# Where the squares of a sublayer's output are summed, and how many feature blocks the sample columns share an operation

## The chip, the cores and the metric

The kernel runs on one core of one Trainium2 chip. Its time is the device time of one launch in microseconds (us), taken as the median of a few runs. PE is TensorE (matrix products), DVE is VectorE, ACT is ScalarE, POOL is GpSimd, SP is SyncE, which only issues transfers here. PSUM is the memory that TensorE writes its products into.

## The reference, cut to what matters

The program is one inference step of a two-layer decoder of width 1024, over a prompt of 512 tokens and a sample group of 8 sequences of 4 tokens. Each layer is a mixer and a convolutional feed-forward network (FFN); around each of these four sublayers stand two RMS norms:

```python
h = _rmsnorm(x, ng[0]) * (1 + sc1) + sh1        # before the sublayer
y, ... = _mixer_ab(h, ...)                      # or _mixer_cd, or _conv_ffn
x = x + g1 * _rmsnorm(y, ng[1])                 # after it
```

`_rmsnorm` multiplies by `rsqrt(mean(x * x, axis=-1) + EPS)`: the mean runs over the 1024 features of a token. `sh1`, `sc1`, `g1` (and three more for the FFN) are one vector for the prompt and one for each sample sequence, so sample columns need another factor than prompt columns.

## The kernel before, in words

Activations lie feature-major: a tile has 128 partitions (features of one of KB = 8 feature blocks), two token halves h = 0 and 1, and HT = 272 columns in each (256 prompt columns and 16 sample columns). A sum over features is therefore a sum over partitions and blocks; it is made by a matmul with `onesD`, a 128x128 matrix whose entries make the mean.

Every large product is made of three matmuls of 272 columns per 128x128 weight block: high part by high part (L618), high weight by low activation (L620), low weight by high activation (L622). `gemm` takes most output blocks with both token halves in one (`ps`, two PSUM banks, two such buffers). At the first blocks after a norm ("lead") and the last blocks of a sublayer ("tail") it goes through half h = 0 of all of them first, and then through h = 1, so that the norm of one half can run beside the products of the other. Of the halved blocks those with number 1, 3 and 6 use a `ps` buffer (in the trace `psmm`), the others a single-bank buffer `p1` (`psmh`), of which there are three. Mixer 0 has four halved tail blocks, FFN 0, mixer 1 and FFN 1 have eight each.

The end of a sublayer is called a junction here. It goes like this for each half:

- `out_evac` takes a block from PSUM. In the FFNs DVE adds it to the partial sum `Yf` (L686). ACT squares it (L694, the first block L689), the square is added to `yacc` (L696): on DVE for blocks of half 0, on POOL for blocks of half 1 and for blocks of both halves. ACT multiplies the prompt columns by the gate (L697), DVE the 16 sample columns (L698).
- `postres` makes one matmul of `yacc` with `onesD` into `psn` (L491). ACT and DVE make 1/sqrt of it (`nr`, L494 to L497), and DVE multiplies the output by it and adds the residual, two blocks per operation (L539, L540).
- `premod` prepares the next sublayer: ACT squares X (L506), eight matmuls sum the squares into `psn` (L491), ACT and DVE multiply by the scale (L518, L519), and after `nr` DVE multiplies by it (L523), adds the shift to the sample columns (L524), ACT writes the rounded high part `Hhi` (L526 for prompt columns, L527 for sample columns) and DVE the low part `Hlo` (L529, L531). The loop takes CH = 2 blocks at a time.

The fourth junction, after the last FFN, has no `premod` behind it; its second half ends the program.

The instruction order on each engine comes from a scheduler that takes the program text, its dependences and the buffers; `tc.issue_after(x)` keeps what is inside behind instruction x. `evacuate` puts each `out_evac` behind the newest weight load. What matters for the order is thus which buffer a matmul needs and what frees it: a block can't start until an earlier block of its buffer has been read by DVE or ACT.

Of the kernel before, what the change touches and what calls it, by code (L numbers as in the profile page):

```python
# [13 lines left out]
P = 128  # L14
# [5 lines left out]
HT = 272  # L20
# [247 lines left out]
def build(nc, tc, ctx, t):  # L268
# [214 lines left out]
        w = np_.tile([P, 1], F32, name="warm")  # L483
        A.activation(w, x, AF.Abs_reciprocal_sqrt, bias=epsb)

    def rstd(parts, ones):

        ps = pp.tile([P, 512], F32, name="psn", tag="pn", bufs=1)[:, :HT]
        n = len(parts)
        for i, a in enumerate(parts):  # L490
            PE.matmul(ps, ones, a, start=(i == 0), stop=(i == n - 1))  # L491
        r = np_.tile([P, HT], F32, name="nr", bufs=2)
        q = np_.tile([P, HT], F32, name="nq", bufs=2)
        A.activation(r, ps, AF.Abs_reciprocal_sqrt, bias=epsb)  # L494
        V.scalar_tensor_tensor(q, r, -0.5, r, op0=M, op1=M)
        V.scalar_tensor_tensor(q, ps, EPS, q, op0=ADD, op1=M)
        V.scalar_tensor_tensor(r, q, 1.5, r, op0=ADD, op1=M)  # L497
        return r

    CH = 2  # L500

    def squares(h):
        parts = []
# [6 lines left out]
    def premod(l, s, h, tmp):  # L510

        ca, sh = cA[l][s], mods[l][:, 24 * s:24 * s + 8, :]
        parts = squares(h)
        ws = []
        for c in range(0, KB, CH):
            w = tmp(c, CH)
            for k in range(CH):
                A.activation(w[:, k, 0:256], X[:, c + k, h, 0:256], AF.Copy, scale=ca[:, c + k, 0:1])  # L518
            V.tensor_tensor(s44(w), s44(X[:, c:c + CH, h, :]), bmod(ca, c, c + CH, h), op=M)  # L519
            ws.append(w)  # L520
        r = rstd(parts, onesD)
        for w, c in zip(ws, range(0, KB, CH)):
            V.tensor_tensor(w, w, r.unsqueeze(1).to_broadcast([P, CH, HT]), op=M)  # L523
            V.tensor_tensor(s44(w), s44(w), bmod(sh, c, c + CH, h), op=ADD)  # L524
            for k in range(CH):
                A.activation(Hhi[:, c + k, h, 0:256], w[:, k, 0:256], AF.Identity, bias=sh[:, c + k, 0:1])  # L526
            A.activation(Hhi[:, c:c + CH, h, 256:272], w[:, :, 256:272], AF.Copy)  # L527
            for k in range(CH):
                V.scalar_tensor_tensor(Hlo[:, c + k, h, 0:256], w[:, k, 0:256], sh[:, c + k, 0:1],  # L529
                                       Hhi[:, c + k, h, 0:256], op0=ADD, op1=SUB)  # L530
            V.tensor_tensor(Hlo[:, c:c + CH, h, 256:272], w[:, :, 256:272], Hhi[:, c:c + CH, h, 256:272], op=SUB)  # L531

    def postres(h, Y, acc, out=None):
        r = rstd([acc[:, h, :]], onesD)
        for c in range(0, KB, CH):
            y = Y[:, c:c + CH, h, :]
            x = X[:, c:c + CH, h, :]
            E = G if c in POOLED else V
            E.tensor_tensor(y, y, r.unsqueeze(1).to_broadcast([P, CH, HT]), op=M)  # L539
            E.tensor_tensor(x, x, y, op=ADD)  # L540
            if out is not None:
                SY.dma_start(out[:, c:c + CH, h, :], x)
# [132 lines left out]
    def out_evac(Y, acc, cg, fresh, final):  # L675

        def ev(i, n, ps, h0, h1):
            y, src = Y[:, n, h0:h1, :], ps[:, h0:h1, :HT]
            if not final:
                if fresh:  # L680
                    A.activation(y, src, AF.Copy)
                else:
                    V.tensor_tensor(y, src, y, op=ADD)
                return
            if not fresh:
                V.tensor_tensor(y, src, y, op=ADD)  # L686
                src = y
            if i == 0:
                A.activation(acc[:, h0:h1, :], src, AF.Square)  # L689
                if h0 == 0:  # L690
                    warm(acc[:, 0, 0:1])
            else:
                sq = np_.tile([P, 2, HT], F32, name="nsq2", tag="nsq", bufs=NSQ)
                A.activation(sq[:, h0:h1], src, AF.Square)  # L694
                E = V if h1 == 1 else G
                E.tensor_tensor(acc[:, h0:h1, :], acc[:, h0:h1, :], sq[:, h0:h1], op=ADD)  # L696
            A.activation(y[:, :, 0:256], src[:, :, 0:256], AF.Copy, scale=cg[:, n, 0:1])  # L697
            V.tensor_tensor(y[:, :, 256:272].rearrange("p a (b t) -> p a b t", t=4),  # L698
                            src[:, :, 256:272].rearrange("p a (b t) -> p a b t", t=4),
                            cg[:, n, 1 + 4 * h0:1 + 4 * h1].rearrange("p (a b) -> p a b", b=4).unsqueeze(3)  # L700
                            .to_broadcast([P, h1 - h0, 4, 4]), op=M)
        return ev

    def yacc():
        return np_.tile([P, 2, HT], F32, name="yacc")


    def ffn(l, nxt, side, pre):
        pre()
        es = ExitStack()  # L710
        fp = es.enter_context(pool(f"ffn{l}"))
        ey, Y = ExitStack(), []

        def open_y():
            Y.append(ey.enter_context(pool(f"ffny{l}", side="right")).tile([P, KB, 2, HT], F32, name="Yf"))

        act_hi = fp.tile([P, 7, 2, HT], F32R, name="act_hi")
        act_lo = fp.tile([P, 7, 2, HT], F32R, name="act_lo")
        so = fp.tile([P, FB, 9, 2], F32, name="fso")
        if l == 0:  # L720
            apool.append((fp, ADB[1]))
        exts = [fp.tile([P, 562], F32, name=f"fext{i}") for i in range(FEXT)]
        SY.dma_start(so, t[f"st_f{l}"])
        for e in exts:
            G.memset(e[:, 0:2], 0.0)
        wo, bo = PAR["f_w"][0] + l * 132, PAR["f_b"][0] + l * 44
        acc = yacc()
        zs, live, cnt = {}, {}, [0]

        def up_ev(i, nb, ps, h0, h1):  # L730
            if h0 == 0:
                live[nb] = exts[cnt[0] % FEXT]
                cnt[0] += 1
                fill_state(live[nb], 2, so[:, nb, 1:9])
            ext = live[nb]
            A.activation(fpr(ext, 2, h0, h1), cpr(ps, h0, h1), AF.Copy)  # L736
            V.tensor_copy(fsa(ext, 2, 6, 2, h0, h1), csa(ps, h0, h1))  # L737
            if h1 != 2:
                return
            save_state(ext, 2, so[:, nb])  # L740
            z = fp.tile([P, 562], F32, name="fz", bufs=4)
            conv3(z, ext, par[:, wo + 3 * nb:wo + 3 * nb + 3], par[:, bo + nb:bo + nb + 1])
            zs[nb] = z
            if nb < NF:
                return
            n = nb - NF
            za, zg = zs.pop(n), zs.pop(nb)
            A.activation(zg[:, :560], zg[:, :560], AF.Silu)
            V.tensor_tensor(za[:, :560], za[:, :560], zg[:, :560], op=M)
            hi, lo = act_hi[:, n % 7], act_lo[:, n % 7]  # L750
            split(fpr(za, 0), cpr(hi), cpr(lo))
            split(zsa(za), csa(hi), csa(lo))

        def ups(n0, n1):
            return [x for n in range(n0, n1) for x in (n, NF + n)]

        def up(n0, n1, **k):
            return gemm(ups(n0, n1), srcH, up_ev, **k)

        def down(gi):  # L760
            b0, b1 = FGROUPS[gi]
            fin = gi == len(FGROUPS) - 1
            return gemm(range(KB), lambda k: (act_hi[:, (b0 + k) % 7], act_lo[:, (b0 + k) % 7]),
                        out_evac(Y[0], acc, cG[l][1], gi == 0, fin), tail=TAILF if fin else 0,
                        mids=(None, lambda: junction(0, Y[0], acc, nxt)))

        def body():
            ng = len(FGROUPS)
            yield from up(0, FGROUPS[0][1], lead=LEADF)
            open_y()  # L770
            for gi in range(ng - 1):
                e = FGROUPS[gi][1]
                yield from up(e, e + 1)
                yield from down(gi)
                yield from up(e + 1, FGROUPS[gi + 1][1])
            for i, _ in enumerate(down(ng - 1)):
                if i == 3:
                    with queued():
                        SY.dma_start(t[f"o_f{l}"], so)
                yield  # L780
            del apool[1:]

        weave(body(), side)
        es.close()
        return lambda: (junction(1, Y[0], acc, nxt), ey.close())
# [4 lines left out]
    def mixer0(nxt, side, begun):  # L790
# [1 line left out]
        mp = es.enter_context(pool("mix0"))  # L792
        yhi = mp.tile([P, KB, 2, HT], F32R, name="yhi")
        ylo = mp.tile([P, KB, 2, HT], F32R, name="ylo")
        acc = yacc()
        ea = ExitStack()
        ap_ = ea.enter_context(pool("mix0a"))
        oa = ap_.tile([P, 4, 9, 2], F32, name="oa")
# [98 lines left out]
    def mixer1(nxt, pre):  # L897
        pre()
        es = ExitStack()
        tp = es.enter_context(pool("mix1t"))  # L900
        acc = yacc()
        qs = tp.tile([P, 3, 2, 2, P], F32, name="qs")
        ks = tp.tile([P, 6, 32], F32, name="ks")
        vnew = tp.tile([P, 256], F32, name="vnew")
# [521 lines left out]
```

## Time and profile before

| what | value |
|---|---|
| median of 3 runs | 1440.73 us (1440.14 to 1442.59) |
| profiled execution | 1443.65 us, span of its instructions 1441.6 us |
| mean granted TensorE clock in it | 0.982 of full |
| PE busy | 1378.7 us, 96% of the span |
| DVE busy | 873.6 us, 61% |
| ACT busy | 609.1 us, 42% |
| POOL busy | 117.4 us, 8% |

Busy times are summed over the span, and engines overlap, so they don't add up to it. "Idle before, releaser" in a row is how long the engine stood still ahead of that instruction, and which other engine's instruction let it go on. PEclk is the clock that TensorE was granted as a share of full speed, 2.4 GHz; 0.50 is its lower level, 1.2 GHz. Times in rows with a start count from the start of the span.

### The profile page before, as it was taken

To read this page: it belongs to the slowest core of one execution; us is meant where nothing else is said; L and a number is where in the kernel's file an instruction comes from. 1 tells how busy PE (TensorE), PEld (TensorE's weight loads), DVE (VectorE), ACT (ScalarE), POOL (GpSimd) and SP (SyncE) were. 2 spreads that over 40 slices of the span, in tenths; PEclk is the share of its full clock that TensorE was granted. 3 is DMA by queue.
4 is the path that set the end of the run, shared out by engine and by line. 5 is a ranking of instruction groups with operands and counts; after the bars stand their busy time and mean duration, and the time that the engine had idled before them with its cause. 6 is when DMAs were issued, how large, how long until landed. Compare 5 with 4: busy or idle time off the path is not lost.

```text
span 1441.6 us, 27411 instructions
## 1 busy us (share of the span) xinstructions
PE 1378.7 (96%) x10762; PEld 1281.2 (89%) x10762; DVE 873.6 (61%) x1830; ACT 609.1 (42%) x1148; POOL 117.4 (8%) x354
## 2 busy tenths in 40 slices
PE   6999999999999999998899999899899999999995
PEld 4789998999999999988899998577799999999995
DVE  4743359652554464368689888536886257366467
ACT  4421357442442343257433433536654344244244
POOL 0100012100100010003000000000221011011001
PEclk9999999999999999999999999999899999999998
DMA  9666413344535444442443131554142533655821
GB/s 353 245 206 215 159 61 111 112 147 141 160 95 191 149 138 132 147 158 60 132 94 102 49 112 60 176 208 147 46 129 81 184 116 125 224 192 186 275 83 62
DMA packets 111016, 207.73 MB, mean 144 GB/s; under 512 B 19332, under 2 KB 32132, under 8 KB 110376
## 3 DMA queue, kind: packets, MB, share of 16 engines
q1 hardware_dynamic: 109088, 202.58, 43.2%
q10 hardware_dynamic: 1800, 3.42, 0.7%
q8 instruction: 84, 1.38, 0.4%
q14 instruction: 44, 0.36, 0.1%
HBM read 198.63 MB, written 34.39 MB: 162 GB/s over the span
## 4 chain that ended last, share of the span: by engine, by line
PE 89%; DVE 6%; ACT 2%; DMA 2%; issue 1%; POOL 0%; POOLq 0%; SPq 0%; DVEq 0%; ACTq 0%
PE psmm L618 24%; PE psmm L620 23%; PE psmm L622 23%; PE psada L432 3%; PE psn L491 3%; PE psmh L618 2%; PE psmh L620 2%; PE psmh L622 1%; PE pso L1116 1%; PE psl L1082 1%; PE psl L1084 1%; DVE wlo L559 1%; DVE X L540 1%; DMA kc<-kc 1%; PE pssm L1168 1%
## 5 line engine op out<-in xcount | busy, mean ns | idle before, releaser
L618 PE MATMUL psmm<-Hhi,whi 128*128 128x272 f32 x2028 | 436.3, 292 | 0.0
L622 PE MATMUL psmm<-Hhi,wlo 128*128 128x272 f32 x2028 | 429.4, 289 | 0.0
L620 PE MATMUL psmm<-Hlo,whi 128*128 128x272 f32 x2028 | 428.8, 289 | 0.0
L558 ACT ACTIVATE whi<-wraw 128x512 fp32r<-128x512 f32 (+1 forms) x404 | 234.2, 598 | 389.6 <-PE psmm L620 349.8
L559 DVE TENSOR_TENSOR wlo<-wraw,whi 128x512 fp32r<-128x512 f32 (+1 forms) x404 | 257.1, 651 | 202.1 <-ACT whi L558 194.4
L618 PEld LDWEIGHTS psmm<-Hhi,whi 128*128 128x128 f32 x2028 | 322.1, 189 | 22.3 <-issue 12.8
L622 PEld LDWEIGHTS psmm<-Hhi,wlo 128*128 128x128 f32 x2028 | 322.7, 189 | 1.4 <-issue 1.4
L620 PEld LDWEIGHTS psmm<-Hlo,whi 128*128 128x128 f32 x2028 | 322.0, 188 | 1.5 <-issue 1.4
L618 PE MATMUL psmm<-act_hi,whi 128*128 128x272 f32 x624 | 134.5, 291 | 0.0
L622 PE MATMUL psmm<-act_hi,wlo 128*128 128x272 f32 x624 | 133.2, 288 | 0.0
L620 PE MATMUL psmm<-act_lo,whi 128*128 128x272 f32 x624 | 133.0, 288 | 0.0
L736 ACT ACTIVATE fext<-psmm 128x512 f32<-128x512 f32 (+1 forms) x88 | 50.2, 571 | 148.1 <-PE psmm L622 148.1
L668 DVE SCALAR_TENSOR_TENSOR fz<-fext,par,fz 128x560 f32<-128x560 f32 x88 | 70.5, 801 | 56.8 <-ACT fz L667 56.1
L618 PEld LDWEIGHTS psmm<-act_hi,whi 128*128 128x128 f32 x624 | 99.0, 188 | 6.7 <-ACT whi L558 4.1
L622 PEld LDWEIGHTS psmm<-act_hi,wlo 128*128 128x128 f32 x624 | 99.2, 188 | 0.9 <-issue 0.8
L620 PEld LDWEIGHTS psmm<-act_lo,whi 128*128 128x128 f32 x624 | 99.2, 188 | 0.5 <-issue 0.4
L977 DVE SCALAR_TENSOR_TENSOR zd<-extd,par,zd 128x512 f32<-128x512 f32 x120 | 86.9, 747 | 1.0 <-ACT zd L967 0.3
L667 ACT ACTIVATE fz<-fext,par 128x560 f32<-128x560 f32 x88 | 75.0, 853 | 24.9 <-DVE fext L737 24.2
L669 DVE SCALAR_TENSOR_TENSOR fz<-fext,par,fz 128x560 f32<-128x560 f32 x88 | 70.4, 800 | 2.1
L737 DVE COPY fext<-psmm 128x32 f32<-128x32 f32 (+1 forms) x88 | 16.5, 187 | 90.7 <-ACT fext L736 89.5
L659 POOL COPY fso<-fext 128x2 f32<-128x2 f32 x88 | 20.4, 232 | 536.9 <-ACT fext L736 536.9
L432 PE MATMUL psada<-adaw,cact 128*32 128x256 f32 x768 | 57.4, 392 | 0.3 <-DMA adaw<-ada_w 0.3
(264 smaller groups left out, 1661.9 us busy)
## 6 DMA issues: line engine op xcount, KB each, us to landing
adaw<-ada_w SPq DMA_DIRECT2D x96, 512.0 KB, 4.1
wraw<-w_up SPq DMA_DIRECT2D x176, 256.0 KB, 3.3
wraw<-w_dn SPq DMA_DIRECT2D x64, 256.0 KB, 3.4
o_c<-cache SPq DMA_DIRECT2D x8, 2040.0 KB, 9.2
wraw<-w_cdi SPq DMA_DIRECT2D x52, 256.0 KB, 3.1
wraw<-w_abi SPq DMA_DIRECT2D x32, 256.0 KB, 6.3
o_c<-cache SPq DMA_DIRECT2D x8, 1016.0 KB, 6.6
kc<-kc SPq DMA_DIRECT2D x28, 256.0 KB, 3.7
```

Of the source, the lines that this page charges most:

```text
L432: PE.matmul(ps[32 * j:32 * j + 32, :], cact[:, k, :], wt[:, j // 2, 256 * (j % 2):256 * (j % 2) + 256], start=(k == 0), stop=(k == KB - 1))
L491: PE.matmul(ps, ones, a, start=(i == 0), stop=(i == n - 1))
L558: newest["ACT"] = A.activation(hi[:, :n], raw[:, :n], AF.Copy).ins
L559: newest["DVE"] = V.tensor_tensor(lo[:, :n], raw[:, :n], hi[:, :n], op=SUB).ins
L618: PE.matmul(ps[:, h, :HT], whi, xhi[:, h, :], start=(i == 0), stop=False)
L620: PE.matmul(ps[:, h, :HT], whi, xlo[:, h, :], start=False, stop=False)
L622: x = PE.matmul(ps[:, h, :HT], wlo, xhi[:, h, :], start=False, stop=(i == last))
L667: A.activation(z[:, :n], ext[:, 2:2 + n], AF.Identity, bias=b, scale=w[:, 2:3])
L668: V.scalar_tensor_tensor(z[:, :n], ext[:, 1:1 + n], w[:, 1:2], z[:, :n], op0=M, op1=ADD)
L669: V.scalar_tensor_tensor(z[:, :n], ext[:, 0:n], w[:, 0:1], z[:, :n], op0=M, op1=ADD)
L736: A.activation(fpr(ext, 2, h0, h1), cpr(ps, h0, h1), AF.Copy)
L977: V.scalar_tensor_tensor(cpr(z), ip, dw[:, i:i + 1], cpr(z), op0=M, op1=ADD)
```

## The change

The squares of an output block that is evacuated by halves are no longer added up by DVE or POOL. They stay in their `nsq2` buffer, and TensorE adds them over partitions by a matmul with `onesD` into a PSUM bank `psq`, one matmul for each block and half (`flush_squares`, L722 and L723 of the changed kernel), one block later than they are made. The bank is one of the three `p1` buffers, taken at the second block of a half and held until `rstd` has read it. `postres` no longer makes the `psn` matmul. Squares of blocks with both halves (the first four of mixer 0) are added by DVE to `acc["t"]`, which goes in by one more matmul per half. The table load of ACT (`warm`) moves ahead of the first square. In `premod` the sample columns go four blocks per operation (CJ = 4), and the order of DVE's and ACT's operations in a group changes.

```diff
-    def rstd(parts, ones):
+    def rstd(parts, ones, ps=None):
+        if ps is None:
+            ps = pp.tile([P, 512], F32, name="psn", tag="pn", bufs=1)[:, :HT]
 ...
+    CJ = 4
 ...
-        for c in range(0, KB, CH):
-            w = tmp(c, CH)
-            for k in range(CH):
+        for c in range(0, KB, CJ):
+            w = tmp(c, CJ)
+            for k in range(CJ):
                 A.activation(w[:, k, 0:256], X[:, c + k, h, 0:256], AF.Copy, scale=ca[:, c + k, 0:1])
-            V.tensor_tensor(s44(w), s44(X[:, c:c + CH, h, :]), bmod(ca, c, c + CH, h), op=M)
+            V.tensor_tensor(s44(w), s44(X[:, c:c + CJ, h, :]), bmod(ca, c, c + CJ, h), op=M)
             ws.append(w)
         r = rstd(parts, onesD)
-        for w, c in zip(ws, range(0, KB, CH)):
-            V.tensor_tensor(w, w, r.unsqueeze(1).to_broadcast([P, CH, HT]), op=M)
-            V.tensor_tensor(s44(w), s44(w), bmod(sh, c, c + CH, h), op=ADD)
-            for k in range(CH):
+        for w, c in zip(ws, range(0, KB, CJ)):
+            for a in range(0, CJ, CH):
+                V.tensor_tensor(w[:, a:a + CH], w[:, a:a + CH], r.unsqueeze(1).to_broadcast([P, CH, HT]), op=M)
+            V.tensor_tensor(s44(w), s44(w), bmod(sh, c, c + CJ, h), op=ADD)
+            A.activation(Hhi[:, c:c + CJ, h, 256:272], w[:, :, 256:272], AF.Copy)
+            for k in range(CJ):
                 A.activation(Hhi[:, c + k, h, 0:256], w[:, k, 0:256], AF.Identity, bias=sh[:, c + k, 0:1])
-            A.activation(Hhi[:, c:c + CH, h, 256:272], w[:, :, 256:272], AF.Copy)
-            for k in range(CH):
+            V.tensor_tensor(Hlo[:, c:c + CJ, h, 256:272], w[:, :, 256:272], Hhi[:, c:c + CJ, h, 256:272], op=SUB)
+            for k in range(CJ):
                 V.scalar_tensor_tensor(Hlo[:, c + k, h, 0:256], ...)
-            V.tensor_tensor(Hlo[:, c:c + CH, h, 256:272], w[:, :, 256:272], Hhi[:, c:c + CH, h, 256:272], op=SUB)

     def postres(h, Y, acc, out=None):
-        r = rstd([acc[:, h, :]], onesD)
+        flush_squares(acc, True)
+        r = rstd(None, None, acc[h])
 ...
-            if i == 0:
-                A.activation(acc[:, h0:h1, :], src, AF.Square)
-                if h0 == 0:
-                    warm(acc[:, 0, 0:1])
+            if i == 0 and h0 == 0:
+                warm(src[:, 0, 0:1])
+            flush_squares(acc)
+            if h1 - h0 == 2 and "t" not in acc:
+                acc["t"] = np_.tile([P, 2, HT], F32, name="yacc")
+                A.activation(acc["t"], src, AF.Square)
             else:
                 sq = np_.tile([P, 2, HT], F32, name="nsq2", tag="nsq", bufs=NSQ)
                 A.activation(sq[:, h0:h1], src, AF.Square)
-                E = V if h1 == 1 else G
-                E.tensor_tensor(acc[:, h0:h1, :], acc[:, h0:h1, :], sq[:, h0:h1], op=ADD)
+                if h1 - h0 == 2:
+                    V.tensor_tensor(acc["t"], acc["t"], sq, op=ADD)
+                else:
+                    acc["next"] = (h0, sq[:, h0])
 ...
+    def flush_squares(acc, last=False):
+        if "next" not in acc:
+            return
+        h, sq = acc.pop("next")
+        fresh = h not in acc
+        if fresh:
+            acc[h] = psum1("psq")[:, :HT]
+        with tc.issue_after(newest["PE"]):
+            if fresh and "t" in acc:
+                PE.matmul(acc[h], onesD, acc["t"][:, h, :], start=True, stop=False)
+            PE.matmul(acc[h], onesD, sq, start=fresh and "t" not in acc, stop=last)
```

What the scheduler makes of it is shown at three places. First, PE in the last FFN's output product, half 0, where the last block of activations is waited for. Before, five blocks (15817 is block 0) had done nine of their twelve matmuls when the wait comes; these rows begin with the last of those 45 and go on with the first five that need the last activations:

```order
L622 MATMUL psmh_15918<-act_hi_11364,wlo_15820 128x272
L618 MATMUL psmh_15817<-act_hi_11364,whi_15673 128x272
L618 MATMUL psmm_15848<-act_hi_11364,whi_15679 128x272
L618 MATMUL psmh_15879<-act_hi_11364,whi_15743 128x272
L618 MATMUL psmm_15898<-act_hi_11364,whi_15749 128x272
L618 MATMUL psmh_15918<-act_hi_11364,whi_15819 128x272
L620 MATMUL psmh_15817<-act_lo_11365,whi_15673 128x272
```

In the changed kernel three blocks stand there (27 matmuls), and the others come behind:

```order
L626 MATMUL psmm_15853<-act_hi_11318,wlo_15703 128x272
L622 MATMUL psmh_15770<-act_hi_11318,whi_15626 128x272
L622 MATMUL psmm_15802<-act_hi_11318,whi_15632 128x272
L622 MATMUL psmm_15853<-act_hi_11318,whi_15702 128x272
L624 MATMUL psmh_15770<-act_lo_11319,whi_15626 128x272
L626 MATMUL psmh_15770<-act_hi_11318,wlo_15627 128x272
```

Two blocks, 18 matmuls, have moved from ahead of the wait to behind it. Second, DVE at the same junction, where half 0's `postres` (L539 and L540, of the changed kernel L543 and L544) meets the evacuations of half 1 (L686, L690). Before:

```order
L686 TENSOR_TENSOR Yf_12262<-psmh_16014,Yf_12262 128x272
L698 TENSOR_TENSOR Yf_12262<-Yf_12262,cG11_94 128x16
L686 TENSOR_TENSOR Yf_12262<-psmm_16031,Yf_12262 128x272
L495 SCALAR_TENSOR_TENSOR nq_15997<-nr_15996 128x272
L496 SCALAR_TENSOR_TENSOR nq_15997<-psn_15994,nq_15997 128x272
L698 TENSOR_TENSOR Yf_12262<-Yf_12262,cG11_94 128x16
L497 SCALAR_TENSOR_TENSOR nr_15996<-nq_15997,nr_15996 128x272
L686 TENSOR_TENSOR Yf_12262<-psmh_16050,Yf_12262 128x272
L539 TENSOR_TENSOR Yf_12262<-Yf_12262,nr_15996 128x2x272 x2
```

And in the changed kernel, from `nr` of half 0 on:

```order
L690 TENSOR_TENSOR Yf_12215<-psmh_15968,Yf_12215 128x272
L497 SCALAR_TENSOR_TENSOR nq_15951<-psq_15828,nq_15951 128x272
L498 SCALAR_TENSOR_TENSOR nr_15950<-nq_15951,nr_15950 128x272
L706 TENSOR_TENSOR Yf_12215<-Yf_12215,cG11_94 128x16
L543 TENSOR_TENSOR Yf_12215<-Yf_12215,nr_15950 128x2x272 x2
L544 TENSOR_TENSOR X_67<-X_67,Yf_12215 128x2x272 x2
L543 TENSOR_TENSOR Yf_12215<-Yf_12215,nr_15950 128x2x272 x2
L544 TENSOR_TENSOR X_67<-X_67,Yf_12215 128x2x272 x2
L690 TENSOR_TENSOR Yf_12215<-psmm_15986,Yf_12215 128x272
L690 TENSOR_TENSOR Yf_12215<-psmh_16006,Yf_12215 128x272
```

Before, the evacuations of blocks 0, 1 and 2 of half 1 stand ahead of `postres`; now block 0's alone does, and block 1's (15986) and all later ones stand behind its eight operations. Third, PE at that place in the changed kernel: block 6 of half 1 is 16082, which takes the buffer of block 1, 16025 is block 3, 16063 block 5:

```order
L624 MATMUL psmm_16082<-act_lo_11319,whi_15804 128x272
L626 MATMUL psmm_16082<-act_hi_11318,wlo_15805 128x272
L622 MATMUL psmm_16082<-act_hi_11318,whi_15804 128x272
L723 MATMUL psq_16000<-nsq2_16002,onesD_79 128x272
L723 MATMUL psq_16000<-nsq2_16021,onesD_79 128x272
L622 MATMUL psmh_16063<-act_hi_11318,whi_15778 128x272
L624 MATMUL psmh_16063<-act_lo_11319,whi_15778 128x272
L626 MATMUL psmh_16063<-act_hi_11318,wlo_15779 128x272
```

The first matmul of block 6, one row ahead of these, waits for DVE's evacuation of block 1, and the squares 16002 and 16021 are those of blocks 1 and 2. Behind these rows come the rest of blocks 5, 6 and 7 and the other five `psq` matmuls, in the kernel before the end of PE's work was one `psn` matmul behind the same blocks.

## Rows read from the trace of the kernel before

**Rows 1.** Windows, the four junctions: length, busy us (instructions) by engine, granted clock.

```profile
187.00:236.00 49.00, 46.44 (x325) 43.14 (x324) 34.76 (x86) 30.63 (x74) 6.79 (x13) 1.00 0.22 67
642.00:699.00 57.00, 48.23 (x319) 42.85 (x320) 44.66 (x118) 39.24 (x97) 12.49 (x18) 0.92 0.23 69
...
988.00:1038.00 50.00, 39.94 (x233) 35.73 (x232) 43.96 (x115) 37.99 (x92) 6.62 (x7) 0.83 0.20 64
1404.00:1441.60 37.60, 21.00 (x156) 19.50 (x154) 27.50 (x68) 15.73 (x37) 5.88 (x7) 0.85 0.17 60
```

**Rows 2.** Windows after a wait of PE; the column behind POOL is its clock.

```profile
698.00:703.00 5.00, 4.70 (x19) 4.47 (x20) 5.00 (x18) 3.63 (x12) 0.00 (x0) 0.50 0.00 0
...
1406.00:1412.00 6.00, 5.84 (x45) 5.78 (x46) 4.21 (x15) 4.04 (x9) 0.00 (x0) 1.00 0.01 3
```

**Rows 3.** Timeline of PE in mixer 1's tail: start, us, line, tiles.

```profile
997.41 0.29 PE L622 MATMUL psmh<-Hhi,wlo 128*128 128x272 f32 x1
997.54 0.62 PE L491 MATMUL psn<-yacc,onesD 128*128 128x272 f32 x2
997.80 0.49 PE L618 MATMUL psmh<-Hhi,whi 128*128 128x272 f32 x1
998.13 0.29 PE L620 MATMUL psmh<-Hlo,whi 128*128 128x272 f32 x1
```

**Rows 4.** Timeline of PE after the wait at 1017.39.

```profile
1017.39 0.60 PE L618 MATMUL psmh<-Hhi,whi 128*128 128x272 f32 x1 [6.15 <-ACT Hhi L527]
...
1022.08 0.43 PE L622 MATMUL psmh<-Hhi,wlo 128*128 128x272 f32 x1
1022.30 0.43 PE L618 MATMUL psmh<-Hhi,whi 128*128 128x272 f32 x1
```

**Rows 5.** Line L696 by engine: count, min/median/max ns, first and last start.

```profile
L696 POOL TENSOR_TENSOR yacc<-yacc,nsq x28: 755/916/1363, 175.3 to 1429.2; 128x272 f32<-128x272 f32 x25, 128x544 f32<-128x544 f32 x3
...
L696 DVE TENSOR_TENSOR yacc<-yacc,nsq x25: 429/441/445, 190.5 to 1414.9; 128x272 f32<-128x272 f32 x25
```

**Rows 6.** Timeline of DVE, premod of the second junction, half 0 and half 1.

```profile
668.84 2.39 DVE L523 TENSOR_TENSOR Yf<-Yf,nr 128x544 f32<-128x544 f32 x2
671.16 0.74 DVE L524 TENSOR_TENSOR Yf<-Yf,mod 128x32 f32<-128x32 f32 x1
...
696.41 1.36 DVE L523 TENSOR_TENSOR Yf<-Yf,nr 128x544 f32<-128x544 f32 x2
697.68 0.18 DVE L524 TENSOR_TENSOR Yf<-Yf,mod 128x32 f32<-128x32 f32 x1
```

**Rows 7.** Timeline of POOL in the second junction.

```profile
667.62 4.23 POOL L696 TENSOR_TENSOR yacc<-yacc,nsq 128x272 f32<-128x272 f32 x4 [29.66 <-ACT nsq L694]
```

**Rows 8.** Timeline of PE in the second junction.

```profile
655.15 0.72 PE L491 MATMUL psn<-yacc,onesD 128*128 128x272 f32 x2
...
673.48 0.59 PE L620 MATMUL psmh<-Hlo,whi 128*128 128x272 f32 x1 [0.69 <-DVE Hlo L531]
...
698.30 0.60 PE L618 MATMUL psmh<-Hhi,whi 128*128 128x272 f32 x1 [3.88 <-ACT Hhi L527]
```

**Rows 9.** Timeline of PE at the end of the kernel.

```profile
1406.16 0.39 PE L618 MATMUL psmh<-act_hi,whi 128*128 128x272 f32 x1 [1.60 <-DVE act_hi L672]
...
1415.37 0.72 PE L491 MATMUL psn<-yacc,onesD 128*128 128x272 f32 x2
...
1430.02 1.03 PE L491 MATMUL psn<-yacc,onesD 128*128 128x272 f32 x2 [4.46 <-POOL yacc L696]
```

**Rows 10.** Timeline of DVE at the end of the kernel, from postres of half 0.

```profile
1419.05 1.34 DVE L539 TENSOR_TENSOR Yf<-Yf,nr 128x544 f32<-128x544 f32 x2
...
1424.79 0.43 DVE L686 TENSOR_TENSOR Yf<-psmm,Yf 128x272 f32<-128x272 f32 x1
```

**Rows 11.** Timeline of ACT at the end of the kernel.

```profile
1408.28 0.43 ACT L694 ACTIVATE nsq<-Yf 128x272 f32<-128x272 f32 x1
1408.72 1.28 ACT L484 ACT_TABLE_LOAD   x1
```

More of the change, by code (lines that the diff above doesn't have):

```diff
@@ L484, in warm @@
         A.activation(w, x, AF.Abs_reciprocal_sqrt, bias=epsb)
-    def rstd(parts, ones):
[L488 to L491, printed above, removed]
+    def rstd(parts, ones, ps=None):
+        if ps is None:
+            ps = pp.tile([P, 512], F32, name="psn", tag="pn", bufs=1)[:, :HT]
+            n = len(parts)
+            for i, a in enumerate(parts):
+                PE.matmul(ps, ones, a, start=(i == 0), stop=(i == n - 1))
         r = np_.tile([P, HT], F32, name="nr", bufs=2)
@@ L702, in out_evac @@
         return ev
-    def yacc():
-        return np_.tile([P, 2, HT], F32, name="yacc")
+    def flush_squares(acc, last=False):
[9 more added lines that the diff above has]
+            PE.matmul(acc[h], onesD, sq, start=fresh and "t" not in acc, stop=last)
     def ffn(l, nxt, side, pre):
@@ L726, in ffn @@
         wo, bo = PAR["f_w"][0] + l * 132, PAR["f_b"][0] + l * 44
-        acc = yacc()
+        acc = {}
         zs, live, cnt = {}, {}, [0]
@@ L794, in mixer0 @@
         ylo = mp.tile([P, KB, 2, HT], F32R, name="ylo")
-        acc = yacc()
+        acc = {}
         ea = ExitStack()
@@ L900, in mixer1 @@
         tp = es.enter_context(pool("mix1t"))
-        acc = yacc()
+        acc = {}
         qs = tp.tile([P, 3, 2, 2, P], F32, name="qs")
```

## Prediction

> **What bounds the kernel now.** I read the share of busy time by engine first: PE works in 96% of the span, so outside the four junctions nothing that DVE, ACT or POOL lose can show, and the change touches nothing there. I then cut windows around the junctions [rows 1]. The first, mixer 0 to FFN 0, leaves PE idle for 49.00 − 46.44 = 2.56 us, the second for 8.8 us, the third for 10.1 us, and the last 37.6 us hold only 21.0 us of PE. So each junction is a race between PE and the chain from the last square to the next activations (sum, `nr`, DVE, next matmul), and the reader should ask of each edit which of the two it lengthens.
>
> A wait of PE costs more than itself. After the 3.88 us wait at 698.30 [rows 8] the granted clock is 0.50, the 1.2 GHz level, for the five microseconds shown; after the 1.60 us wait at 1406.16 [rows 9] it stays 1.00 [rows 2]. At full clock a 272-column matmul follows its forerunner by 0.13 us [rows 3], at the lower level by 0.22 [rows 4].
>
> **What is added: 58 matmuls on PE.** Two halves times 5, 8, 8 and 8 make 58 `psq` matmuls; eight `psn` matmuls on `yacc` go, 50 net. Their price is read where PE had no wait: from 997.41 to 998.13 [rows 3] there are three steps, two of which are ordinary (0.13 each), so the matmul with `onesD` takes 0.72 − 0.26 = 0.46 us. Where it has to wait it occupies 0.72 [rows 8]. At no cover the change costs PE 50 × 0.46 = 23 us; if idle time hides them all, nothing. The junctions decide.
>
> **What is removed.** DVE loses 25 additions of 0.44 us and POOL 28 of 0.92 us [rows 5]. POOL's matter more than their own time. From 667.62 on four of them run for 4.23 us [rows 7], and DVE's pair of multiplications at 668.84 beside them takes 2.39 us and the shift 0.74, against 1.36 and 0.18 at 696.41 with POOL still [rows 6]: 1.6 us on the chain of half 0 that would go. The Trainium skill ("SBUF — State Buffer", section "Who interferes with whom") says that VectorE with two SBUF inputs and GpSimd exclude each other at a shared port, and the trace agrees with its direction here: 2.39 against 1.36. The fewer sample operations of CJ = 4 take two small DVE operations of 0.18 us each off three places of a half; they may be lost again, since the first Hlo block now waits for a copy and a shift of four blocks. I count this part at −0.4 to +0.4 us a half, zero in the sum.
>
> **Junction 1: +1.** Half 0 gains some 2 us by POOL's silence; PE gets 10 `psq` matmuls and loses two, 8 × 0.46 = 3.7 us, against 2.56 us of idle time [rows 1]. The difference is +1.1; I take +1, with −1 (half 1 starts earlier by the gain) to +2 as its bounds.
>
> **Junction 2: −3.** Half 0 has 8 `psq` in PE's own stream, so the sum of its squares is complete about 4.5 us later than the end of the `psn` matmul, 655.87 [rows 8]: eight times 0.46 less the 0.72 that goes, and more since the bank that `psq` holds leaves two instead of three for blocks, so that matmuls of half 1 no longer stand ready to be put between. From there to the first full matmuls of the next mixer it was 673.48 − 655.87 = 17.6 us. That chain now loses 1.6 us to the contention that goes, and three evacuations (0.43 each, as in [rows 10]) that stood in DVE's queue between `psn` and the products move behind, 1.3, and some 0.9 of additions: 13.8 us. So PE's restart is at 655.87 + 4.5 + 13.8 = 674.2, 0.7 later. What changes is half 1: it comes with more work for PE and a shorter chain, and the wait of 3.88 us at 698.30 should shrink to one that doesn't lower the clock. Five microseconds at 0.50 [rows 2] lose 2.5; the wait is worth up to 3.9; 14 × 0.46 = 6.4 us of new work is to be paid out of 8.8 us of idle time. I take −3; the bounds are −5 (all goes) and +1.5 (the wait stays and half 0's delay runs through).
>
> **Junction 3: −0.5.** The same work, but half 0's next activations come late whatever is done: the wait of 6.15 us at 1017.39 [rows 4] follows squares, sum and multiplications. Half 0's sum is later by 8 × 0.46 less some overlap, and the chain shorter by the contention. The low clock, from 1017.39 to past 1022.30 [rows 4], may end earlier if PE has more to do. From −4 to +2.5, −0.5 taken.
>
> **The end: +7.** Here nothing follows that could hide work, and the order gets worse. First, only 27 matmuls stand ahead of the wait for the last activations where 45 did, because one bank belongs to `psq`. PE, which stood still 1.60 us at 1406.16 [rows 9], stands still 1.60 + 18 × 0.126 = 3.9 us and has 18 more matmuls behind it. The first `psq` comes then behind a square that stands behind ACT's table load, 1.28 us, while before a square stood ahead of it [rows 11]; I put it at about 1410. From there to the last `psq` of half 0 are 56 matmuls and eight `psq`: 56 × 0.126 + 8 × 0.46 = 10.7, so 1420.7 against the end of `psn` at 1416.09 [rows 9].
>
> Second, `postres` of half 0 takes DVE 5.74 us, from 1419.05 to 1424.79 [rows 10], and by its order only block 0 of half 1 has been evacuated ahead of it. Its start follows the sum by 2.96 us before; without one of the evacuations and the small operations some 2.2, so it goes from 1422.9 to 1428.6. PE has 55 matmuls and one `psq` to do meanwhile (7.4 us, to 1428.1) and then needs the `ps` buffer of block 1. Behind that evacuation (0.43 us) PE has 36 matmuls and seven `psq`: 4.5 + 3.2 = 7.7 us, and the last square hangs on the last block, an evacuation and a square of 0.43 us each [rows 10, 11], of which about half lies beside the matmuls: 1429.0 + 7.7 + 0.5 = 1437.2. Before, the last sum ended at 1430.02 + 1.03 = 1431.05 [rows 9]; the gain there is that POOL's adds and the slow matmul at the low clock go, and it is in the sum. That makes +6.2 at full clock.
>
> Third, the clock. A wait of 3.9 us is as long as the one at 698.30 after which it was 0.50. The low clock would stretch the 18 matmuls to 18 × 0.22 = 4.0 us, to 1410.3, where `psq` had to wait until about 1410 anyway, and slow what follows for a microsecond or two: +1 at most 1.5. The Trainium skill ("TensorE: Matmul & The Clock Gate", section "HAM oscillation — how this bites in real kernels") describes just this, matmul groups between waits that start again at half clock; by it the end is +7.2, without it +6.2. I take +7; the bounds are +3.5 (the evacuations get in ahead of `postres`' chain, since ACT and DVE have less to do) and +9 (low clock to the end).
>
> **The sum.** 1 − 3 − 0.5 + 7 = +4.5 us. The profiled execution took 1443.65 us (span 1441.6), so it would take 1448.2; it lies 2.92 us above the median 1440.73, and against the median the forecast is 1445.2.
>
> **Rivals.** (a) Idle time hides the new matmuls and the freed engines win: POOL's silence and 11 us less on DVE shorten each chain, the low-clock stretches at the second and third junction go. Price: −1, −5, −3, and at the end +3.5: −5.5, 1435.2 us. For it speak 8.8 and 10.1 us of idle PE [rows 1]; against it that half 0's sums wait for PE's own queue, which is full until then, and the end, where nothing is idle that helps. (b) The terms cancel: the second and third junction give −5 and −2, the first 0, the end +7 at full or low clock: 1440.7. For it speaks that the gains are where PE waits longest. (c) The other end: PE is the bound in all junctions, as it is in the first, since `psq` matmuls wait for squares in PE's queue with ready matmuls behind them; each new wait is paid in full. Then between half and all of 50 × 0.46 us shows, 1452 to 1464 us. It decides from the point where a square is later than the next block's matmuls; against it stands that the square is used a block late, 12 × 0.126 = 1.5 us, against 0.43 + 0.43 for evacuation and square.
>
> **How the numbers follow.** The forecast, +3 to +9, has a chance of 0.48; (a) 0.23; (b) 0.22; (c) 0.07. About 0.2%, 2.9 us, is what a measurement of this kernel can tell: (a) counts as faster, (b) as no change; of the forecast's own cases a small part falls to within 0.2%. So faster 0.23, same 0.24, slower 0.53. The range: from 1436, which leaves the better half of (a) out, to 1452, which leaves (c) out.
>
> **What the changed profile would show.** In the last part, a wait of some 3.9 us ahead of the first matmul of the last activations, clock 0.50 or not behind it; `postres` of half 0 starting at about 1423 in before's time, one evacuation ahead of it; a wait of PE for DVE behind block 4 of half 1, and the last `psq` near 1437. In the second junction, the pair of multiplications at 1.36 instead of 2.39 in half 0 and a wait below 3 us for half 1, with the clock at 1.00. `psq` rows of 0.46 us a step. The forecast is wrong if the wait for half 1 stays at the second junction (it is then slower than forecast), or if DVE reaches blocks 1 to 3 of half 1 before `postres` needs `nr`, or the third junction loses its low clock altogether (then it is faster).

## The result and the profile after

The changed kernel takes 1453.9 us (median of 5 runs, 1452.68 to 1455.23) against 1441.42 for the one before in the same runs: ratio 1.0084, 95% interval 1.0073 to 1.0095. It is 12.5 us slower. The forecast had the sign right but said 4.5 us, and 1453.9 lies above the range's end of 1452.

Where the time went is read by the start of the same matmul in both traces. (The profiled executions have spans of 1453.4 and 1441.6 us, 11.8 apart.) All numbers of the table are us; a plus means that the changed kernel is later.

| place | start before | difference there | share of the part ahead of it | forecast |
|---|---|---|---|---|
| behind junction 1 | 244.9 | −0.1 | −0.1 | +1 |
| behind junction 2 | 750.4 | +2.2 | +2.3 | −3 |
| ahead of junction 3 | 969.9 | +2.1 | −0.1 | 0 |
| behind junction 3 | 1065.9 | +3.7 | +1.6 | −0.5 |
| ahead of the end | 1391.3 | +3.5 | −0.2 | 0 |
| end of the span | 1441.6 | +11.8 | +8.3 | +7 |

One trace against another is uncertain by two or three microseconds in such a table: kernels with the same code up to the end differ by as much ahead of it (below), and the trace of the kernel before is of an execution of 1443.65 us, 2.2 above its median. So the end came out near its forecast. The second junction, where a gain of 3 was forecast, lost 2.3, which is outside its bounds of −5 to +1.5. The third lost 1.6 where 0.5 was to be gained, inside its bounds and within that uncertainty.

The windows of the changed kernel, laid round the same work as those of [rows 1], and one behind the wait at the end (columns as there):

```profile
187.00:236.00 49.00, 48.85 (x339) 45.52 (x338) 32.47 (x77) 30.70 (x74) 2.11 (x8) 1.00 0.22 66
642.00:703.00 61.00, 55.00 (x353) 47.25 (x353) 39.20 (x100) 37.50 (x92) 4.99 (x11) 0.97 0.20 64
668.00:674.00 6.00, 4.23 (x16) 2.79 (x16) 4.56 (x10) 5.95 (x14) 0.00 (x0) 1.00 0.17 47
...
990.00:1042.00 52.00, 44.15 (x264) 38.39 (x262) 39.31 (x100) 39.10 (x91) 0.00 (x0) 0.97 0.20 61
1407.50:1453.40 45.90, 31.98 (x197) 29.03 (x197) 24.50 (x61) 16.63 (x37) 0.00 (x0) 0.85 0.14 49
1409.50:1415.00 5.50, 5.14 (x20) 4.84 (x21) 2.45 (x9) 1.84 (x6) 0.00 (x0) 0.50 0.00 1
```

In the first, PE is busy for 48.85 of 49 us: its idle time took up the new matmuls, and the table shows no loss there. In the second the clock is 0.97 instead of 0.92, DVE and POOL do less, and yet PE has six idle microseconds left in 61. They lie elsewhere than before. PE in the second junction:

```profile
668.53 2.13 PE L492 MATMUL psn<-nsq,onesD 128*128 128x272 f32 x8 [2.13 <-ACT nsq L508]
671.23 2.10 PE L492 MATMUL psn<-nsq,onesD 128*128 128x272 f32 x8 [0.56 <-ACT nsq L508]
674.22 0.73 PE L723 MATMUL psq<-nsq,onesD 128*128 128x272 f32 x2 [0.90 <-ACT nsq L700]
...
703.14 0.39 PE L622 MATMUL psmh<-Hhi,whi 128*128 128x272 f32 x1 [0.94 <-ACT Hhi L528]
```

The wait for half 1's activations has shrunk from 3.88 us [rows 8] to 0.94, as forecast. But from 666.4 to 674.2 PE stands still three times: ahead of each group of four of `premod`'s eight `psn` matmuls (a matmul with `onesD` is two rows of the trace, so a group is x8), and then ahead of half 1's first `psq`. Before, these `psn` matmuls lay between blocks of half 1; now there is no block to put there. The square that the first `psq` waits for is late on ACT and not on DVE: DVE has evacuated block 0 of half 1 at 663.80, ahead of `postres`, but ACT squares it behind the squares and multiplications of `premod`:

```profile
663.80 0.43 DVE L690 TENSOR_TENSOR Yf<-psmh,Yf 128x272 f32<-128x272 f32 x1
...
671.62 1.69 ACT L520 ACTIVATE Yf<-X,cA 128x256 f32<-128x256 f32 x4
...
673.75 0.74 ACT L700 ACTIVATE nsq<-Yf 128x272 f32<-128x272 f32 x2
```

Half 0 of the same junction is late too. The wait for the last activations of FFN 0 at 642.35 has 27 matmuls ahead of it instead of 36 (counted in the two traces), is 1.81 us long instead of 0.68, and is followed by a clock of 0.50 where it was 1.00. PE and a window behind the wait, in the kernel before:

```profile
642.35 0.40 PE L618 MATMUL psmh<-act_hi,whi 128*128 128x272 f32 x1 [0.68 <-DVE act_hi L672]
...
644.00:647.00 3.00, 3.00 (x33) 1.53 (x26) 2.01 (x7) 2.86 (x6) 0.00 (x0) 1.00 0.67 250
```

And in the changed kernel:

```profile
642.35 0.39 PE L622 MATMUL psmh<-act_hi,whi 128*128 128x272 f32 x1 [1.81 <-DVE act_hi L676]
...
644.00:647.00 3.00, 3.00 (x18) 2.27 (x11) 0.96 (x4) 1.73 (x5) 0.00 (x0) 0.50 0.61 226
```

In e2 and e9 below, where 36 stand there, the wait is 0.69 and the same window has 1.00.

At the end PE shows three waits:

```profile
1409.69 0.60 PE L622 MATMUL psmh<-act_hi,whi 128*128 128x272 f32 x1 [3.85 <-DVE act_hi L676]
...
1434.08 0.39 PE L622 MATMUL psmm<-act_hi,whi 128*128 128x272 f32 x1 [0.48 <-DVE Yf L690]
...
1442.13 0.73 PE L723 MATMUL psq<-nsq,onesD 128*128 128x272 f32 x2 [0.54 <-ACT nsq L700]
```

Against 1406.16 [rows 9] plus the 3.5 us that were lost ahead of it, the first matmul of the last activations comes at the same time, but with a wait of 3.85 instead of 1.60 us ahead of it: 18 matmuls that had filled it now stand behind. The clock behind it is 0.50 for all of the window 1409.5 to 1415. DVE in the same stretch:

```profile
1428.50 1.36 DVE L543 TENSOR_TENSOR Yf<-Yf,nr 128x544 f32<-128x544 f32 x2
...
1433.59 0.43 DVE L690 TENSOR_TENSOR Yf<-psmm,Yf 128x272 f32<-128x272 f32 x1
```

`postres` of half 0 starts at 1428.50 (1419.05 before, [rows 10]) and block 1 of half 1 is evacuated behind it, at 1433.59; PE's 1434.08 waits for that.

### The profile page after: what moved, and what is told of

It is laid out like the page before. It is cut to its first block, busy times and chain, and to the rows that moved or that the text cites. A ratio compares the mean times of both kernels' runs of the same rounds, so it can differ in the third digit from the quotient of the medians.

```text
span 1453.4 us, 27473 instructions
## 1 busy us (share of the span) xinstructions
PE 1397.2 (96%) x10862; PEld 1295.4 (89%) x10862; DVE 857.1 (59%) x1772; ACT 609.7 (42%) x1136; POOL 90.2 (6%) x326
## 4 chain that ended last, share of the span: by engine, by line
PE 90%; DVE 5%; ACT 2%; DMA 1%; issue 1%; DVEq 0%; SPq 0%; ACTq 0%
PE psmm L622 24%; PE psmm L624 23%; PE psmm L626 23%; PE psada L432 3%; PE psn L492 2%; PE psq L723 2%; PE psmh L622 2%; PE psmh L624 2%; PE psmh L626 1%; PE pso L1134 1%; PE psl L1100 1%; PE psl L1102 1%; DVE Yf L543 1%; DVE X L544 1%; PE pssm L1186 1%
## 5 line engine op out<-in xcount | busy, mean ns | idle before, releaser
L626 PE MATMUL psmm<-Hhi,wlo 128*128 128x272 f32 x2028 | 428.3, 288 | 0.0
L626 PEld LDWEIGHTS psmm<-Hhi,wlo 128*128 128x128 f32 x2028 | 322.0, 188 | 1.4 <-issue 1.4
L626 PE MATMUL psmm<-act_hi,wlo 128*128 128x272 f32 x624 | 134.4, 290 | 0.0
L626 PEld LDWEIGHTS psmm<-act_hi,wlo 128*128 128x128 f32 x624 | 100.4, 190 | 1.0 <-issue 0.8
```

What stands on the lines that cost most here:

```text
L626: x = PE.matmul(ps[:, h, :HT], wlo, xhi[:, h, :], start=False, stop=(i == last))
```

## The experiments

Each ratio is to the kernel before, from runs on the same chip, with its 95% interval. Four theories were put against one another. A: the `psq` bank, one of the three that half blocks use, keeps blocks from being started ahead of the waits. B: the 50 matmuls of 0.46 us on PE. C: the `premod` of four blocks. Later A was split: A1, the place in the order at which the bank is asked for; A2, the number of banks left.

| kernel | median us | ratio | interval |
|---|---|---|---|
| changed kernel | 1453.9 | 1.0084 | 1.0073 to 1.0095 |
| e1, new premod alone | 1441.56 | 0.9993 | 0.9983 to 1.0003 |
| e2, psq in the bank of psn | 1439.25 | 0.9980 | 0.9970 to 0.9989 |
| e3, psq in one pass | 1444.03 | 1.0015 | 1.0004 to 1.0025 |
| e4, e2 and e3 together | 1432.24 | 0.9928 | 0.9912 to 0.9945 |
| e5, bank held, additions as before | 1454.49 | 1.0080 | 1.0067 to 1.0094 |
| e6, e5 in the bank of psn | 1441.05 | 0.9992 | 0.9983 to 1.0001 |
| e7, yacc in the last FFN | 1447.08 | 1.0034 | 1.0022 to 1.0047 |
| e8, premod of before | 1453.31 | 1.0078 | 1.0064 to 1.0092 |
| e9, bank taken at the fifth block | 1437.65 | 0.9973 | 0.9963 to 0.9983 |
| e10, e9 in one pass | 1430.29 | 0.9919 | 0.9906 to 0.9933 |
| e11, e9 with yacc in the last FFN | 1436.51 | 0.9962 | 0.9950 to 0.9975 |

### e1 and e8: is it the new premod?

e1 is the kernel before with `premod` of the changed one; e8 is the changed kernel with `premod` of before (the `premod` part of the diff, done alone and undone alone).

> The kernel before with only the new premod: sample columns of four blocks per operation and its changed order; squares are added by DVE and POOL as before. If the loss of 12.5 us comes from the squares on TensorE (theories A and B below), this run takes 1441.4 plus or minus 2 us. Theory C, that the later first Hlo block of a group of four holds up the next sublayer, expects 1444 to 1449 us, the loss at the second and third junction (some 2 us each).

Measured 0.9993. C falls: no loss. Its trace shows about 2 us less at the second junction; the median doesn't show them.

> The changed kernel with the premod of before (two blocks per operation). Alone, the new premod was within the measurement's uncertainty (ratio 0.9993), though its profile shows 2.1 us less at the second junction. If that gain is real in the changed kernel, this run is 1 to 3 us above the changed one (ratio to before 1.009 to 1.011); if the second junction is bound by PE's missing blocks, it is the same within 1 us.

Measured 1.0078, within the interval of the changed kernel's 1.0084. Grouping four blocks changes nothing that these runs can tell, in either kernel.

### e2 to e4: the bank, or the time on PE?

```diff
-            acc[h] = psum1("psq")[:, :HT]
+            acc[h] = pp.tile([P, 512], F32, name="psq", tag="pn", bufs=1)[:, :HT]
```

> The changed kernel with one edit: psq takes the bank of psn instead of one of the three p1 banks. Theory A, that the loss comes from the bank (blocks can no longer be started ahead of the waits), expects half of the loss or more back: 1445 to 1448 us, and a wait of PE for the last activations of FFN 1 back near 1.6 us instead of 3.85. Theory B, that the loss is the time of 50 matmuls of 0.46 us on a full PE, expects 1452 to 1454 us: the bank is only a place.

Measured 0.9980: not half of the loss came back but all of it and a little more, 1.04% or 15.0 us. PE in e2 behind the wait for the last activations of FFN 1, where it had been 3.85 us:

```profile
1399.55 0.39 PE L622 MATMUL psmh<-act_hi,whi 128*128 128x272 f32 x1 [1.60 <-DVE act_hi L676]
```

and the window of the second junction in which the changed kernel's PE had stood still:

```profile
666.00:674.00 8.00, 8.00 (x51) 7.23 (x51) 7.48 (x20) 7.95 (x22) 0.00 (x0) 1.00 0.22 66
```

PE is busy for all of these 8 us; the changed kernel has it busy for 4.23 of 6 there.

```diff
-                PE.matmul(acc[h], onesD, sq, ...)
+                PE.matmul(acc[h], onesR, sq, ...)      # onesR and sq are fp32r
```

> The changed kernel with the squares of half blocks and onesD in fp32r, so that a psq matmul is one pass; the bank stays p1. The squares are rounded a little. Theory B expects 58 x (0.46 - 0.13) = 19 us less work on PE, of which the part on the path comes back: 1440 to 1446 us. Theory A expects 1450 to 1453 us, since blocks still can't start ahead.

Measured 1.0015, inside B's bounds. In the trace of e4 a `psq` matmul in one pass follows and is followed at the ordinary 0.13 us:

```profile
1402.55 0.29 PE L623 MATMUL psmm<-act_hi,whi 128*128 128x272 f32 x1
1402.67 0.29 PE L724 MATMUL psq<-nsq,onesR 128*128 128x272 f32 x1
1402.80 0.29 PE L625 MATMUL psmm<-act_lo,whi 128*128 128x272 f32 x1
```

So 56 × 0.33 = 18 us less work on PE (the two matmuls that take `acc["t"]` stay as they are) gave 0.69%, 9.9 us.

> Both edits: psq in the bank of psn and in one pass. If A and B each hold for a part, the gains add up and the kernel is at or below the one before: 1436 to 1441 us, with DVE and POOL relieved. If something else costs the time (C, or DVE's postres ahead of the evacuations at the end), it stays above 1444.

Measured 0.9928. Within the intervals the two edits add up: the bank is worth 0.87% with one pass (e3 to e4) and 1.04% with two, the pass 0.69% with the bank held and 0.52% without. Both A and B hold, each for its own part, and the bank's is the larger.

### e5 and e6: the bank without the matmuls

The kernel before, in which only the first half block's square goes into `psq` at the second block, and the sum of the others at the end; 8 matmuls more than before.

```diff
+            if half and ("first", h0) in acc and h0 not in acc:
+                acc[h0] = psum1("psq")[:, :HT]
+                with tc.issue_after(newest["PE"]):
+                    PE.matmul(acc[h0], onesD, acc["first", h0], start=True, stop=False)
 ...
+        PE.matmul(acc[h], onesD, acc["t"][:, h, :], start=False, stop=True)    # in postres
```

> The kernel before, additions on DVE and POOL and premod unchanged, but the first half block's square goes into a psq bank of the p1 buffers by one matmul at the second block, and the sum of the others goes in by one matmul in postres: the bank is held as long as in the changed kernel, with 8 matmuls more than before instead of 50 (at most 3.7 us). Theory A, the held bank costs most of the loss: 1448 to 1454 us, with 27 matmuls ahead of the wait at the end. Theory B, the work on PE: 1441 to 1445 us.

Measured 1.0080: as much as the whole loss of the changed kernel, without its 50 matmuls. The places agree in part: by the traces e5 loses 2.3 us at the second junction, 5.0 at the third and 4.1 at the end, the changed kernel 2.3, 1.6 and 8.3. At the second junction its trace shows the same waits of PE, the one for the last activations of FFN 0, then those for the `psn` matmuls and half 1's first `psq`:

```profile
642.99 0.40 PE L620 MATMUL psmh<-act_hi,whi 128*128 128x272 f32 x1 [1.81 <-DVE act_hi L674]
...
666.78 2.13 PE L492 MATMUL psn<-nsq,onesD 128*128 128x272 f32 x8 [3.03 <-ACT nsq L507]
669.47 2.10 PE L492 MATMUL psn<-nsq,onesD 128*128 128x272 f32 x8 [0.56 <-ACT nsq L507]
672.47 0.72 PE L694 MATMUL psq<-nsq,onesD 128*128 128x272 f32 x2 [0.90 <-ACT nsq L698]
```

> Control of the run before: the same two matmuls per half, but in the bank of psn. Theory A expects the time of the kernel before plus at most the 8 matmuls, 1441 to 1445 us, so 5 us or more below its twin; theory B expects no difference between the twins.

Measured 0.9992, 0.88% or 12.7 us below its twin, from the same matmuls in another bank. PE at the same places:

```profile
641.95 0.39 PE L620 MATMUL psmh<-act_hi,whi 128*128 128x272 f32 x1 [0.69 <-DVE act_hi L674]
...
662.66 2.13 PE L492 MATMUL psn<-nsq,onesD 128*128 128x272 f32 x8
665.50 2.00 PE L492 MATMUL psn<-nsq,onesD 128*128 128x272 f32 x8
...
669.12 0.70 PE L694 MATMUL psq<-nsq,onesD 128*128 128x272 f32 x2
```

No wait stands ahead of `psn` or `psq`.

### e7: the last FFN as before

In `ffn`, `acc` of the last layer is the `yacc` of before; the additions are again on DVE and POOL there.

> The changed kernel, but in the last FFN the squares are added up in yacc by DVE and POOL as before. The profile puts 8.3 of the 11.8 us of the loss into the end of the kernel; if that place is right and independent of the rest, this run is 7 to 9 us below the changed kernel: ratio to before 1.002 to 1.004, 1444 to 1448 us.

Measured 1.0034, so 0.50% or 7.2 us less than the changed kernel, just inside what was expected. Its trace has 3.1 us more than before ahead of the end (the changed kernel 3.5) and 3.6 at the end of the span: the place is right, and 0.34% remain for the junctions.

### e9: the same bank, asked for later

The squares of the first four half blocks wait in their buffers, two to a buffer, and `psq` is taken from the same three banks when the fifth block is evacuated.

```diff
-        if "next" not in acc:
+        q = acc.get("next", [])
+        if not q or (not last and q[0][0] not in acc and len(q) < LATEQ):    # LATEQ = 4
             return
 ...
```

> The changed kernel with psq still in a p1 bank, but asked for later: the squares of the first four half blocks wait in their buffers, and the bank is taken at the fifth block, so that five blocks stand ahead of the wait for the last activations again. Theory A1, that the loss is the place in the order at which the bank is asked for (later blocks can't take a p1 bank before psq has): most of the loss comes back, 1441 to 1445 us. Theory A2, that it is the number of banks left while psq holds one: less than half comes back, 1448 to 1453 us, since the bank is still held over the second part of each half and the squares come in a burst at its end.

Measured 0.9973, below both bounds, 1.11% or 16 us below the changed kernel. The bank is still one of the three and still held until `nr` is made, and costs nothing that can be seen. But e9 holds it for a shorter time too: behind the first junction it is 9 to 14 us from the first `psq` matmul to the last reading, in the changed kernel 10 to 17. What parts A1 from A2 is the count at the end. If only the number of banks mattered, `psq` would take one of three and leave two, for blocks 0 and 2; with blocks 1 and 3, which lie in the `ps` buffers, 36 matmuls would stand ahead of the wait. The changed kernel's trace has 27, nine `psmh` and 18 `psmm`: block 2, whose request comes behind `psq`'s, isn't started although a bank is left for it. In e9 the 45 of before stand there again (27 `psmh`, 18 `psmm`). So A2 explains at most half of the 18 matmuls that moved, and A1 explains them all. (e9 also lays the squares two to a buffer, which was not tried alone; e2 gains as much without it.) The waits in e9's trace:

```profile
642.64 0.39 PE L624 MATMUL psmh<-act_hi,whi 128*128 128x272 f32 x1 [0.69 <-DVE act_hi L678]
...
663.30 2.13 PE L493 MATMUL psn<-nsq,onesD 128*128 128x272 f32 x8
```

and, at the end:

```profile
1396.38 0.39 PE L624 MATMUL psmh<-act_hi,whi 128*128 128x272 f32 x1 [1.60 <-DVE act_hi L678]
```

### e10 and e11: what is left

> The changed kernel with the bank taken at the fifth block (as in the run before) and the squares and onesD in fp32r, one pass instead of two; the squares are rounded a little. If the price of psq matmuls on PE is what is left of theory B, this gains about as much as one pass gained with psq in the bank of psn (7 us): 1430 to 1433 us. If the order was all, 1436 to 1439.

Measured 0.9919, 0.54% below e9, at the lower end of what was expected. With e4, whose interval overlaps, this is the fastest kernel of the study, 11.4 us below the one before, with squares that are rounded to fp32r; where they may not be rounded, e9 and e2 are left.

> The changed kernel with the bank taken at the fifth block, and in the last FFN the squares in yacc by DVE and POOL as before. With the bank asked for late the profile still shows 3.4 us more at the end of the kernel than before, and 9.8 us less ahead of it: if what is left at the end is the squares on PE there, and the junctions don't touch each other, this is 1432 to 1435 us; if the order at the end costs it whoever adds the squares, 1437 to 1439.

Measured 0.9962, 0.11% or 1.6 us below e9, with intervals that overlap: it falls between the two expectations. At its end the trace shows 0.3 us more than before where e9 shows 3.5, as expected; but ahead of it e11 has gained 7.2 us and e9 9.8, with the same code there. Whether the end works back on what is ahead (the order is made over the whole program) or single traces differ by that much, these runs don't tell.

## Why the prediction was wrong

**The step that failed** is the second junction's −3, which came out at +2.3. The prediction named the cause itself, "the bank that `psq` holds leaves two instead of three for blocks, so that matmuls of half 1 no longer stand ready to be put between", but put it into half 0's sum alone (the +4.5). It then assumed that behind this sum only the chain over DVE matters and that PE would be busy in half 1. In fact half 1 asks for its `psq` too, at its second block, and a later block on those banks isn't started before `psq` has had its first matmul. That matmul waits for a square, and the square stands in ACT's queue behind `premod` of half 0 (from 667.82 to 673.36) although its block was evacuated at 663.80. So PE runs out of blocks at 666.4 and gets them back at 674.2. In e2 and e9 ACT squares that block behind `premod` too (at 668.4 and 668.5), but there the blocks don't wait for it. With the bank elsewhere or asked for later the same code gives the second junction −4.5 (e2) and −6.0 (e9) by the traces, so a gain as forecast could be had there (its size is uncertain by the two or three microseconds named above), and was taken by the bank's place in the order. e5 shows that the early request takes as much where the additions are left as before: +2.3 there as well.

The same cause is taken too narrowly in the prediction's other terms. It put 27 matmuls instead of 45 down to the bank that "belongs to `psq`"; that accounts for 36, and the request's place in the order for the rest. And it saw this at the last FFN alone: the wait for FFN 0's last activations, which grew from 0.68 to 1.81 us, is in no term.

Point by point:

- Half 0's sum at the second junction was put 4.5 us later; it ends at 662.88 instead of 655.87, 7.0 later. In e9, with the same eight matmuls, it ends at 657.87, 2.0 later. The 5.0 us between them are the order, as far as the traces show: 1.1 by the longer wait at 642.35, about 1.5 by the clock of 0.50 behind it (an estimate: 3 us at half speed), and 15 more product matmuls ahead of the last `psq`, 15 × 0.126 = 1.9.
- POOL's silence: right. The pair of multiplications beside which POOL added is down from 2.39 [rows 6] to 1.36. In e1, with the new `premod` but POOL's additions, the first three of half 0 still take 1.19 to 1.28 each, where two take 1.36 here, so the new `premod` isn't the reason:

```profile
675.31 1.36 DVE L526 TENSOR_TENSOR Yf<-Yf,nr 128x544 f32<-128x544 f32 x2
```

- The price of a `psq` matmul: right. From L626 to the second row behind the pair are three steps, 0.71 us, of which 0.25 are ordinary: 0.46.

```profile
656.38 0.29 PE L626 MATMUL psmh<-act_hi,wlo 128*128 128x272 f32 x1
656.50 0.62 PE L723 MATMUL psq<-nsq,onesD 128*128 128x272 f32 x2
656.76 0.49 PE L622 MATMUL psmm<-act_hi,whi 128*128 128x272 f32 x1
657.09 0.29 PE L624 MATMUL psmm<-act_lo,whi 128*128 128x272 f32 x1
```

- The end: the mechanism was right in all three parts. The wait was put at 3.9 and is 3.85; the clock behind it is 0.50; `postres` holds up block 1. By size it is +8.3 against +7, since `postres` starts 2 us later than worked out (1428.5 against 1422.9 + 3.5). The low clock slows all of the stretch to 1415, where 1 us had been counted. Some 5 of these 8.3 us go with the bank again: the same share is +2.4 in e2 and +3.5 in e9. The table load, on the other hand, delayed nothing: it ran while PE waited, and the first square waits for DVE:

```profile
1408.33 1.28 ACT L484 ACT_TABLE_LOAD   x1
1411.76 0.29 ACT L484 ACTIVATE warm<-Yf,epsb 128x1 f32<-128x1 f32 x1 [2.15 <-DVE Yf L690]
1411.96 0.73 ACT L700 ACTIVATE nsq<-Yf 128x272 f32<-128x272 f32 x2
```

- The first junction's +1 came out at −0.1 and the third's −0.5 at +1.6, both within their bounds; what the third junction really lost, one trace can't tell.
- Rival (c) had the time, 1452 to 1464, and not the mechanism: e5 loses as much with 8 new matmuls instead of 50. In part it is true all the same: about half of the work that one pass takes off PE comes back as time (7.5 to 9.9 of 18 us, e3, e4 and e10), so the new matmuls do cost; in e2 and e9 what the change relieves pays for them.
- Rival (a), the freed engines win, is what the change gives without the bank: e2 and e9 are faster than before. How little DVE's and POOL's relief brings against PE's new work is seen from e6 to e2, the same bank and the additions moved: 0.9992 to 0.9980, with intervals that overlap (e2 has the new `premod` too, which moved nothing in e1 and e8). It seems that the work on PE takes back nearly all of it, since with one pass 0.5% more is left; the relief alone was not measured.

By the pairs of runs the loss of 0.84% is thus +1.04% (e2) to +1.11% (e9) for the bank's place in the order, and −0.2% to −0.3% for everything else in the change. The other pairs put the bank at 0.87% (e3 to e4) and 0.88% (e6 to e5).

## What to carry to other kernels

An accumulator that is held over many blocks should not be taken from the buffers that the blocks rotate through, or else as late as possible: where buffers are given out in program order, one whose first write waits for a far result stops all later users, though buffers are free. Count in the order how many instructions stand ready ahead of each long wait, before and after. Here 27 stood there instead of 45 at the last FFN and instead of 36 at FFN 0, and at the second junction none were left for half 1; it has to be looked for at every place of that kind, not only at the one where it was first seen. Moving additions to a nearly full engine cost about what it saved here; make them cheap there first (one pass instead of two was worth 0.5% to 0.7%).

## What the runs showed that was not expected

Holding one of three banks for 9 to 14 us cost nothing measurable (e9); asking for it three blocks earlier cost 1.1%. A wait of PE of 1.81 us was followed by a clock of 0.50 (at 642.35), one of 1.60 us at the end of the kernel before was not [rows 2]. And of 18 us of work taken from an engine that is busy for 96% of the span, 7.5 us (e2 to e4), 7.8 (e9 to e10) and 9.9 (changed kernel to e3) came back as time. Where the other half went was not traced; that it lay beside waits is a guess.
